# Input product of an encoder layer: gating columns first, the four heads as seven block products in two passes

## The chip, the cores and the metric

The kernel runs on one core of a Trainium2 chip. The metric is the device time of one execution in microseconds (us); the median of three runs before is 2069.68 us (2069.62 to 2071.15). Engines are named as the profile names them: PE (TensorE matmuls), PEld (its weight loads), DVE (VectorE), ACT (ScalarE), POOL (GpSimd), SP (SyncE, which issues the DMAs here).

## The reference, cut to what matters

One encoder layer over 1536 tokens (512 of the prompt, 1024 of the sample), width 1024, all in fp32. The change concerns the token mixer and, at its edges, the memory keys and values.

```python
z = rms_norm(x, w) @ w_in                      # 1024 x 3072
q, k, v, g, u, vs = split(z, 4 of 512, 2 of 512)
q, k = rotary(q), rotary(k) / sqrt(128)        # four heads of 128
y = bidir_retention(q, k, v, log_gamma)        # chunks of 128 tokens, state forward and backward
ret_out = silu(g) * layer_norm(y) * ret_gn_w
vs = layer_norm(gelu(vs)) * sgu_norm_w
sgu_out = gelu(u) * (sgu_w @ vs + sgu_b)       # chunks of 128 tokens, four groups
mix = concat(ret_out, sgu_out) @ w_out
x = x + rms_norm(mix, w)                       # then cross attention to a memory, then the FFN
```

## The kernel before, in words

Tokens stand in twelve tiles of 128 (`NT`), the width in eight slices of 128 (`KT`). To keep fp32 accuracy every operand is split into a rounded part `hi` and a rest `lo` (`split`, L135; `split_scaled`, L139: ACT writes `hi`, DVE subtracts for `lo`), and each product is three matmuls, hi·hi, hi·lo, lo·hi (`mm3`, L156). A matmul is 128x128 by 128x512.

The **input product** runs in six chunks of 512 columns: u, vs, then one chunk for each head (its q, k, v, g). A tile of a chunk takes 8 x 3 = 24 matmuls (`z_half`, L234). Tiles 0 to 3 of the u chunk run while the first loads arrive (L243 to L257), then tiles 4 to 7, then `chunk_tiles` (L315) goes tile by tile. The whole transposed x stays on the chip in split form (`xp`, `xu`), and the weights of the next chunk are loaded during the current one.

Work that follows a tile is written as generators: `post_vs` (L346) for the gating, `ret_tile` (L403) for the forward part of retention, `ret_back` (L455) for the backward part, in which a step per tile runs from the last tile to the first. They stand in the list `side`, and `advance` (L183) runs each by one step. `chunk_tiles` calls `advance` twice per tile, once for each half:

```python
            z_half(ps, t, 0)
            ...
            advance()
            z_half(ps, t, 1)
            ...
            g = post(i, t, ps)
            next(g, None)
            advance()
```

so that PE meets the small matmuls of retention after every 12 block matmuls. In `ret_tile` DVE scales the tile by `rs_x` (L407), POOL and DVE do the rotary part (L415, L417, L420), and DVE scales k twice (L430, L431).

After the heads come the memory's values and keys (L525 to L557, 16 blocks of 24 matmuls, with an `advance` every 12), into which the tail of retention runs, and then `project` (L584), the product with `w_out`, which reads the mixer's result back from `mixT` in DRAM. A scheduler places each engine's instructions, so that an instruction may stand earlier than its line.

Of the kernel before, what the change touches and what calls it, by code (L numbers as in the profile page):

```python
# [82 lines left out]
def encoder_kernel(ctx: ExitStack, tc, x, xTp, xTs, mem, memT, norm_w, w_in, lg, small, sgu_nw, sgu_wT,  # L83
# [37 lines left out]
    lgt = const([P, 8], "lgt")  # L121
# [79 lines left out]

    cB, cC, sinT = FB.units
# [4 lines left out]
    u_units = FC.units + FD.units  # L207
    u_t = [u_units[t // 2][:, (t % 2) * 512 : (t % 2) * 512 + 512] for t in range(NT)]
    wk_units = FE.units

    xp, xu, W = [], [], []

    def xTk(k, t):

        if t < 4:
            p, o = xp[k // 2], (k % 2) * 512 + t * P
        else:
            p, o = xu[k], (t - 4) * P
        return p[0][:, o : o + P], p[1][:, o : o + P]

    def load_pairs(src, n):

        out = []
        for i in range(4):
            r = raw.next()
            nc.sync.dma_start(r, src[i])
            hi, lo = pair(RA)
            for j in range(2):
                s = slice(j * 512, (j + 1) * 512)
                split_scaled(r[:, s], nw(n, 2 * i + j), hi[:, s], lo[:, s])  # L230
            out.append((hi, lo))
            yield out

    def z_half(ps, t, a):  # L234
        for k in range(4 * a, 4 * a + 4):
            mm3(ps, xTk(k, t), half(W, k), k == 0, k == KT - 1)
# [4 lines left out]
    raw.slots = steady + wk_units + u_units  # L241
    first = [mm() for _ in range(4)]
    for i in range(4):  # L243
        rx, rw = raw.next(), raw.next()
        ux, uw = pair(RA), pair(RX, RC)
        xp.append(ux)
        W.append(uw)
        for j in range(2) if i == 0 else (None,):
            s = slice(0, D) if j is None else slice(j * 512, (j + 1) * 512)
            nc.sync.dma_start(rx[:, s], xTp[i][:, s])  # L250
            nc.sync.dma_start(rw[:, s], w_in[0, i][:, s])
        for j in range(2):
            s, k = slice(j * 512, (j + 1) * 512), 2 * i + j
            split_scaled(rx[:, s], nw(PRE_MIX, k), ux[0][:, s], ux[1][:, s])
            split(rw[:, s], uw[0][:, s], uw[1][:, s])
            for t in range(4):
                mm3(first[t], xTk(k, t), half(W, k), k == 0, k == KT - 1)  # L257

    ss_x = const([P, NT], "ss_x")

    def x_stats(t0, t1):
        for t in range(t0, t1):
            r = raw.next()
            nc.sync.dma_start(r, x[t])
            A.activation(r, r, AF.Square, accum_out=ss_x[:, t : t + 1])
        s = slice(t0, t1)
        V.tensor_scalar_mul(ss_x[:, s], ss_x[:, s], 1.0 / D)
        rsqrt(rs_x[:, s], ss_x[:, s])

    def u_out(t, ps):  # L270
        A.activation(u_t[t], ps, AF.Gelu_apprx_tanh, scale=rs_x[:, t : t + 1])

    x_stats(0, 4)
    raw.slots, raw.i = steady + wk_units, -1
    for t in range(4):
        u_out(t, first[t])
    first = [mm() for _ in range(4)]
    for k in range(KT):
        r = raw.next()
        nc.sync.dma_start(r, xTs[k])  # L280
        hi, lo = pair(RB, RC)
        split_scaled(r, nw(PRE_MIX, k), hi, lo)
        xu.append((hi, lo))
        for i in range(4):
            mm3(first[i], xTk(k, 4 + i), half(W, k), k == 0, k == KT - 1)
    x_stats(4, 8)
    for i in range(4):
        u_out(4 + i, first[i])
    x_stats(8, NT)
    raw.slots, raw.i = steady, -1  # L290
    nc.sync.dma_start(swT, sgu_wT)
    nc.sync.dma_start(snB, sgu_nw.partition_broadcast(P))
    nc.sync.dma_start(cosT, cst[:, C_COS : C_COS + 512])
    nc.sync.dma_start(sinT, cst[:, C_SIN : C_SIN + 1024])
    nc.sync.dma_start(lgt, lg.partition_broadcast(P))
    colc = const([P, 4], "colc")
    nc.sync.dma_start(colc, cst[:, C_COL : C_COL + 4])


    ss_m = const([P, 4], "ss_m")  # L300
# [199 lines left out]
    for h in range(4):  # L500
        for t0, n in SEQS:
# [11 lines left out]
            if h == 3 and t0 == 0:  # L513
                for p in xp:
                    free(*p)
# [784 lines left out]
```

## Time and profile before, and how to read it

| | before |
|---|---|
| median of 3 runs | 2069.68 us |
| profiled execution: time | 2064.9 us |
| profiled execution: span | 2063.1 us |
| mean granted TensorE clock | 0.998 |
| PE busy | 2030.0 us (98%) |
| DVE / ACT / POOL busy | 1162.3 / 853.7 / 656.2 us |
| input product, first matmul to the first of `project` | 6.0 to 592.8 us, memory keys and values included |

Matmuls are pipelined: a row's duration is longer than the distance to the next start, so the cost of one is read from start to start. A busy PE is not a PE at its peak. A row that ends in brackets says how long the engine sat idle before it and what released it. In groups, "xN | busy, mean ns | idle before, releaser" gives the count, the summed and mean duration, and idle time just before.

### The profile page before, as it was taken

How to read it: one execution, taken by the hardware profiler on the slowest of the kernel's cores; microseconds unless marked ns; L12 is line 12 of the kernel's file. 1: busy time of each engine (PE TensorE's matmuls, PEld its weight loads, DVE VectorE, ACT ScalarE, POOL GpSimd, SP SyncE). 2: the span in 40 equal slices, each digit the busy share in tenths (PEclk: the TensorE clock that was granted, in tenths of full speed). 3: DMA queues.
4: the chain of work that ended last, by engine and by line, in shares of the span. 5: the costliest groups of instructions: out<-in, count | busy, mean ns of one | idle time of the engine just before them, and what ended most of it. 6: DMA issues, size and time to landing. Idle time of an engine off the chain costs nothing. (4 is left out here: it accounts for less than half of the span.)

```text
span 2063.1 us, 28521 instructions
## 1 busy us (share of the span) xinstructions
PE 2030.0 (98%) x10442; PEld 1800.3 (87%) x10442; DVE 1162.3 (56%) x2132; ACT 853.7 (41%) x1663; POOL 656.2 (32%) x597
## 2 busy tenths in 40 slices
PE   8999999999999999999999999999999999999998
PEld 7788888888788888888888999999999999788887
DVE  4235566675424354463667555657565656845756
ACT  7623222233324443353445444445444444433432
POOL 0011122221022200002336666766676664000102
PEclk9999999999999999999999999999999999999999
DMA  8411101023643322242457434445444344845653
GB/s 327 125 38 59 47 17 47 25 60 121 204 133 143 123 92 72 72 143 93 143 184 217 128 109 132 123 127 167 132 116 128 104 129 156 278 144 200 226 179 134
DMA packets 158749, 268.12 MB, mean 130 GB/s; under 512 B 13200, under 2 KB 97552, under 8 KB 158608
## 3 DMA queue, kind: packets, MB, share of 16 engines
q1 hardware_dynamic: 158608, 266.30, 40.5%
q8 instruction: 82, 1.34, 0.3%
q14 instruction: 59, 0.48, 0.1%
HBM read 194.81 MB, written 71.44 MB: 129 GB/s over the span
## 5 line engine op out<-in xcount | busy, mean ns | idle before, releaser
L137 DVE TENSOR_TENSOR ra<-fa,ra 128x512 fp32r<-128x512 f32 (+1 forms) x168 | 166.0, 992 | 124.5 <-ACT ra L136 123.0
L157 PE MATMUL mm<-rx,ra 128*128 128x384 f32 (+1 forms) x600 | 214.6, 358 | 10.5 <-ACT rx L136 6.0
L159 PE MATMUL mm<-rx,ra 128*128 128x384 f32 (+1 forms) x600 | 211.0, 352 | 0.0
L158 PE MATMUL mm<-rx,ra 128*128 128x384 f32 (+1 forms) x568 | 198.0, 349 | 0.0
L136 ACT ACTIVATE ra<-fa 128x512 fp32r<-128x512 f32 (+1 forms) x168 | 107.1, 642 | 177.7 <-PE mm L158 147.6
L137 DVE TENSOR_TENSOR ra<-ra,ra 128x512 fp32r<-128x512 f32 x154 | 147.1, 956 | 52.9 <-ACT ra L136 52.4
L157 PE MATMUL mm<-rc,ra 128*128 128x384 f32 (+1 forms) x504 | 173.0, 343 | 3.2 <-ACT rb L1041 3.2
L158 PE MATMUL mm<-rc,ra 128*128 128x384 f32 (+1 forms) x504 | 172.5, 342 | 0.0
L159 PE MATMUL mm<-rc,ra 128*128 128x384 f32 (+1 forms) x504 | 172.1, 341 | 0.0
L172 POOL TENSOR_TENSOR rs<-rq,neg_half 128x1 f32<-128x1 f32 x96 | 57.9, 604 | 358.8 <-DVE rq L171 301.1
L136 ACT ACTIVATE ra<-ra 128x512 fp32r<-128x512 f32 x154 | 97.1, 631 | 140.5 <-PE mm L158 136.3
L157 PEld LDWEIGHTS mm<-rx,ra 128*128 128x128 f32 x600 | 113.6, 189 | 17.3 <-ACT rx L136 6.0
L159 PEld LDWEIGHTS mm<-rx,ra 128*128 128x128 f32 x600 | 113.4, 189 | 6.5
L158 PEld LDWEIGHTS mm<-rx,ra 128*128 128x128 f32 x568 | 107.1, 189 | 4.8 <-DVE rx L137 0.4
L415 POOL TENSOR_TENSOR fe<-fe,fb 128x128 f32<-128x128 f32 x96 | 51.2, 553 | 181.6 <-DVE fe L407 165.7
L1061 POOL TENSOR_TENSOR rb<-rb,rb 128x384 f32<-128x384 f32 x66 | 96.1, 1463 | 24.9 <-DVE rb L1049 18.1
L157 PEld LDWEIGHTS mm<-rc,ra 128*128 128x128 f32 x504 | 94.8, 188 | 6.7 <-ACT rb L1041 4.2
L159 PEld LDWEIGHTS mm<-rc,ra 128*128 128x128 f32 x504 | 94.6, 188 | 2.7
L158 PEld LDWEIGHTS mm<-rc,ra 128*128 128x128 f32 x504 | 95.0, 188 | 2.0
L157 PE MATMUL mm<-rx,rb 128*128 128x512 f32 x208 | 88.2, 424 | 0.1
L593 POOL TENSOR_TENSOR rx<-fa,rx 128x1024 fp32r<-128x1024 f32 x6 | 14.4, 2404 | 212.6 <-PE sm L731 191.2
L159 PE MATMUL mm<-rx,rc 128*128 128x512 f32 x196 | 76.8, 392 | 0.0
(474 smaller groups left out, 5568.8 us busy)
## 6 DMA issues: line engine op xcount, KB each, us to landing
hs<-rb SPq DMA_DIRECT2D x154, 192.0 KB, 2.4
fb<-hs SPq DMA_DIRECT2D x42, 704.0 KB, 4.2
fa<-in_wgu_dram SPq DMA_DIRECT2D x44, 512.0 KB, 4.0
ra<-in_wgu_dram SPq DMA_DIRECT2D x44, 512.0 KB, 3.6
rx<-in_wd_dram SPq DMA_DIRECT2D x77, 256.0 KB, 4.8
fa<-in_w_in_dram SPq DMA_DIRECT2D x20, 512.0 KB, 4.6
fa<-mixT SPq DMA_DIRECT2D x12, 512.0 KB, 3.6
fc<-x1d SPq DMA_DIRECT2D x12, 512.0 KB, 3.9
```

What stands on the lines that cost most here:

```text
L136: A.activation(hi, src, AF.Copy)
L137: V.tensor_tensor(lo, src, f32(hi), op=ALU.subtract)
L157: T.matmul(ps, lhsT=a[0], rhs=b[0], start=first, stop=False, skip_group_check=more)
L158: T.matmul(ps, lhsT=a[0], rhs=b[1], start=False, stop=False, skip_group_check=more)
L159: T.matmul(ps, lhsT=a[1], rhs=b[0], start=False, stop=last, skip_group_check=more)
L172: G.tensor_tensor(out, t, neg_half[:, :w], op=ALU.pow)
L415: G.tensor_tensor(t2q[:, s], zq[:, 1 - s], sinT[:, o : o + 64].unsqueeze(1).broadcast_to([P, 2, 64]), op=ALU.mult)
L593: G.tensor_tensor(a[1], r, f32(a[0]), op=ALU.subtract)
L1061: G.tensor_tensor(c[n], c[n], gated[n], op=ALU.mult)
```

## The change

The gating columns u and vs become one chunk of 1024 columns. Tiles 0 to 3 run while the loads arrive, into all eight PSUM banks; tiles 4 to 11 follow one at a time with the six matmuls of a slice in pairs (as `project` does), their x tile loaded and split one tile ahead. The split weights of both columns stay on the chip, x does not.

For the heads, x is scaled by its norm, taken in pairs of tiles by halves of the width (blocks a11 to a22), and four block sums are made by POOL; the seven left blocks of each of six pairs are written to DRAM (`make_S`). Then two passes of two heads each run seven products (`ORDER`) over six pairs: 42 units of 12 matmuls per pass. A unit loads its left block from DRAM and splits it (`fetch_z`, `split_z`); `right_z` builds the right block of the next product from quarters of `w_in` that are loaded again each time, through two landing slots (`z_land`). Results are added up in SBUF. In the second pass every other left block's `lo` is made by POOL.

Retention of a pass's two heads runs during what follows: heads 0 and 1 in the second pass, heads 2 and 3 in the memory's keys and values. `point` stands in for `advance`: three after every two units of the second pass, and one every six matmuls in the memory stage, with a new tile at every second point. DVE gives up the scaling of z and the two scalings of k (to ACT), and one of two operations in `ret_back`.

```diff
+    for k in range(KT):
+...
+        split(rx[:, o : o + 512], xf[:, 0:512], xf[:, 512:D])
+        for i in range(2):
+            s = slice(i * 512, (i + 1) * 512)
+            split_scaled(rw[:, s], nw(PRE_MIX, k), W[k][0][:, s], W[k][1][:, s])
             for t in range(4):
+                mm3(first[t][i], (xf[:, t * P : (t + 1) * P], xf[:, 512 + t * P : 640 + t * P]),
+                    [q[:, s] for q in W[k]], k == 0, k == KT - 1)
+    def make_S(j, xs):
+...
+            V.tensor_tensor(r, r, row.unsqueeze(1).broadcast_to([P, KT, P]), op=ALU.mult)
+...
+        G.tensor_tensor(s1, a21, a22, op=ALU.add)
+        G.tensor_tensor(s2, s1, a11, op=ALU.subtract)
+        G.tensor_tensor(s3, a11, a21, op=ALU.subtract)
+        G.tensor_tensor(s4, a12, s2, op=ALU.subtract)
+        yield
+        for n, src in ((1, a11), (2, a12), (4, a22), (5, s1), (6, s2), (7, s3), (3, s4)):
+            nc.sync.dma_start(Sd[n, j], src)
+    ORDER = (1, 5, 6, 4, 7, 2, 3)
+    z_units = [(hp, n, tp) for hp in (1, 2) for n in ORDER for tp in range(6)]
+...
+    z_land = Ring([FA.units[2][:, i * 512 : (i + 1) * 512] for i in range(2)])
+    def split_z(i):
+...
+            if i >= 42 and i % 2:
+                A.activation(hi, Sq[i], AF.Copy)
+                G.tensor_tensor(lo, Sq[i], f32(hi), op=ALU.subtract)
+            else:
+                split(Sq[i], hi, lo)
+    def right_z(hp, n, k):
+        def load(kb, cb):
+            r = z_land.next()
+            nc.sync.dma_start(r, w_in[hp, 4 * kb + k][:, cb * 512 : (cb + 1) * 512])
+            return r
+...
+        if n == 1:
+            A.activation(st, load(0, 0), AF.Identity, scale=n0)
+            split(st, hi, lo)
+        elif n in (5, 6, 4):
+            V.scalar_tensor_tensor(st, load(int(n != 5), int(n != 4)), n0 if n == 5 else n1, st,
+                                   op0=ALU.mult, op1=ALU.subtract)
+            split(st, hi, lo)
+        elif n == 7:
+            r, o = load(1, 1), load(0, 1)
+            A.activation(o, o, AF.Identity, scale=n0)
+            V.scalar_tensor_tensor(r, r, n1, o, op0=ALU.mult, op1=ALU.subtract)
+            split(r, hi, lo)
+        else:
+            split_scaled(load(1, int(n != 2)), n1, hi, lo)
+    for t in range(4, NT):
+...
+                for i in range(2):
+                    T.matmul(pss[i], lhsT=ak[x0], rhs=W[k][x1][:, i * 512 : i * 512 + 512],
+                             start=st and k == 0, stop=sp and k == KT - 1)
-        V.tensor_scalar_mul(z, ps[:, 0:384], rs_x[:, t : t + 1])
-        V.tensor_scalar_mul(kfb[:, 0:P], k, kfs)
-        V.tensor_scalar_mul(kfb[:, P : 2 * P], k, kbs)
+        A.activation(kfb[:, 0:P], k, AF.Identity, scale=kfs)
+        A.activation(kfb[:, P : 2 * P], k, AF.Identity, scale=kbs)
-            V.tensor_scalar(yp, yp, mv[:, 0:1], rs, op0=ALU.subtract, op1=ALU.mult)
-            V.tensor_tensor(yp, yp, sg, op=ALU.mult)
+            V.scalar_tensor_tensor(yp, yp, mv[:, 0:1], sg, op0=ALU.subtract, op1=ALU.mult)
+            A.activation(yp, yp, AF.Identity, scale=rs)
+    for ui, (hp, n, tp) in enumerate(z_units):
+        fetch_z(ui + 2)
+        split_z(ui + 1)
+...
+        if ui in (37, 79):
+...
+            feed[0] = ret_feed(hp)
+        ps = mm()
+        s = Sq.pop(ui)
+        for k in range(4):
+            mm3(ps, (s[:, k * P : (k + 1) * P], s[:, 512 + k * P : 640 + k * P]), Tq[hp, n, k], k == 0, k == 3)
+            if k % 2:
+                credit += 0.75 if ui > 37 else 0.25
+                if credit >= 1.0:
+                    credit -= 1.0
+                    point()
+        if tp < 4 and then[0] < 3:
+            right_z(*then, tp)
+...
+            nxt = load_split(wk[d + 1], (c0[2], rb[8]) if d % 2 == 0 else c0[0:2])
-    project(mixT, w_o, POST_MIX, x, x1d, BLOCKS, Ring([(RA.units[8], RB.units[8]), (RX.units[8], RC.units[8])]),
+    project(mixT, w_o, POST_MIX, x, x1d, BLOCKS, Ring([(RA.units[8], RB.units[8]), (RC.units[2], RC.units[8])]),
```

What the change moves is seen in the order of the instructions. PE, in the retention of one head, before: L157 to L159 are block matmuls of the head's chunk, L435 to L446 the state and score matmuls of one tile, L450 its output, L424 and L425 the transposes of another.

```order
L159 MATMUL mm_2503<-rx2_12_74,rc2_9_71 128x512
L435 MATMUL sm_2548<-fe_17_79,fb_14_76 128x128
L437 MATMUL sm_2548<-fe_17_79,fb_14_76 128x128
L439 MATMUL sm_2548<-fb_14_76,fd_16_78 128x128
L446 MATMUL sm_2523<-fd_16_78,fe_17_79 128x128
L157 MATMUL mm_2556<-rx0_10_72,rb0_4_66 128x512
```

Twelve block matmuls stand from the last of these rows to the output L450 of the same tile. PE in the second pass of the change: L503 is the score of a tile, L149 to L151 block matmuls of a unit, L507 the output of that tile, L481 and L482 the transposes of the next, L532 a backward step.

```order
L503 MATMUL sm_2418<-fc_15_77,fe_17_79 128x128
L149 MATMUL mm_2433<-rx1_19_1357,rc1_8_70 128x512
L150 MATMUL mm_2433<-rx1_19_1357,rc1_8_70 128x512
L151 MATMUL mm_2433<-rx1_19_1357,rc1_8_70 128x512
L149 MATMUL mm_2433<-rx1_19_1357,rc1_8_70 128x512
L150 MATMUL mm_2433<-rx1_19_1357,rc1_8_70 128x512
L151 MATMUL mm_2433<-rx1_19_1357,rc1_8_70 128x512
L532 MATMUL sm_2467<-fe_17_79,fc_15_77 128x128
L507 MATMUL sm_2418<-rc0_20_1383,fe_17_79 128x128
L481 MATMUL sm_2483<-ident_141,fe_17_79 128x128
L482 MATMUL sm_2483<-ident_141,fe_17_79 128x128
```

Here six block matmuls stand between the score and the output; elsewhere in the pass it is twelve, about as often.

DVE in the heads before, one tile's forward work among the backward work of another sequence (L476 to L486):

```order
L407 TENSOR_SCALAR fe_17_79<-mm_2899,rs_x_150 128x384
L476 SCALAR_TENSOR_TENSOR fd_16_78<-sm_2962,dec_1239,fd_16_78 128x128
L417 TENSOR_TENSOR fe_17_79<-fe_17_79,fb_14_76 128x256
L482 SCALAR_TENSOR_TENSOR fb_14_76<-fb_14_76,dec_1239,fd_16_78 128x128
L420 TENSOR_TENSOR fe_17_79<-fe_17_79 128x256
L484 BN_STATS bn6_133_2966<-fd_16_78 128x6
L445 SCALAR_TENSOR_TENSOR fb_14_76<-fb_14_76,dec_1239,sm_2976 128x128
```

DVE in the second pass of the change: L380 and L386 build right blocks from a landed quarter, L136 makes a left block's `lo`, the rest is retention.

```order
L136 TENSOR_TENSOR rc1_8_70<-fb_14_76,rc1_8_70 128x512
L477 TENSOR_TENSOR fe_17_79<-fe_17_79 128x256
L380 SCALAR_TENSOR_TENSOR fa_13_75<-fa_13_75,sml_146 128x512
L502 SCALAR_TENSOR_TENSOR fe_17_79<-fe_17_79,dec_1362,sm_2655 128x128
L505 TENSOR_TENSOR fe_17_79<-sm_2627,fb_14_76 128x128
L474 TENSOR_TENSOR fe_17_79<-rc0_20_1383,fb_14_76 128x256
L510 SCALAR_TENSOR_TENSOR fd_16_78<-sm_2655,dec_1362,fd_16_78 128x128
L477 TENSOR_TENSOR fe_17_79<-fe_17_79 128x256
L386 SCALAR_TENSOR_TENSOR fa_13_75<-fa_13_75,sml_146 128x512
L136 TENSOR_TENSOR rc1_8_70<-fe_17_79,rc1_8_70 128x512
L505 TENSOR_TENSOR fe_17_79<-sm_2672,fb_14_76 128x128
```

The score's mask (L505, between L503 and L507 on PE) now stands in one queue behind the right blocks (L380, L386), which wait for a DMA, and the left blocks' `lo` (L136), for which the next units wait.

## Rows read from the trace of the kernel before

**Rows 1.** The page: span, and busy time of each engine.

```profile
span 2063.1 us, 28521 instructions
PE 2030.0 (98%) x10442; PEld 1800.3 (87%) x10442; DVE 1162.3 (56%) x2132; ACT 853.7 (41%) x1663; POOL 656.2 (32%) x597
```

**Rows 2.** Busy time by stage: gating, heads, inside the heads, memory; last clock, DMA.

```profile
core 0: us, PE busy (x) PEld busy (x) DVE busy (x) ACT busy (x) POOL busy (x), PEclk, DMA share, GB/s
6.00:165.00 159.00, 155.38 (x734) 128.66 (x735) 63.59 (x138) 90.87 (x138) 15.30 (x16) 0.99 0.47 165
165.00:505.00 340.00, 338.27 (x1800) 286.51 (x1799) 212.62 (x669) 97.65 (x303) 74.14 (x136) 1.00 0.15 44
200.00:425.00 225.00, 225.00 (x1206) 191.46 (x1205) 140.79 (x447) 59.00 (x194) 49.67 (x93) 1.00 0.11 32
505.00:592.60 87.60, 85.35 (x382) 68.96 (x381) 38.34 (x81) 27.95 (x38) 9.12 (x10) 1.00 0.63 204
```

**Rows 3.** Timeline of PE, block matmuls: first and last of 37 starts (start, duration).

```profile
59.74 0.39 PE L157 MATMUL mm<-rx,rb 128*128 128x512 f32 x1
...
67.90 0.39 PE L157 MATMUL mm<-rx,rc 128*128 128x512 f32 x1
```

**Rows 4.** Timeline of PE where the vs chunk's first gating matmuls start.

```profile
84.67 0.39 PE L159 MATMUL mm<-rx,ra 128*128 128x512 f32 x1
88.45 1.69 PE L362 MATMUL sm<-fe,fb 128*128 128x128 f32 x8 [3.40 <-ACT fe L356]
89.80 0.77 PE L157 MATMUL mm<-rx,ra 128*128 128x512 f32 x1
...
92.43 0.39 PE L157 MATMUL mm<-rc,ra 128*128 128x512 f32 x1
```

**Rows 5.** Timeline of PE, all idle rows from 500 to 592.

```profile
516.64 0.46 PE L475 MATMUL sm<-fb,fd 128*128 128x128 f32 x2 [0.60 <-DVE fb L482]
523.70 0.46 PE L475 MATMUL sm<-fb,fd 128*128 128x128 f32 x2 [0.62 <-DVE fb L482]
527.20 0.49 PE L475 MATMUL sm<-fb,fd 128*128 128x128 f32 x2 [0.17 <-DVE fb L482]
534.45 0.30 PE L465 MATMUL sm<-ident,fd 128*128 128x128 f32 x1 [0.73 <-DVE fd L490]
```

**Rows 6.** Groups of DVE and ACT up to 640 us.

```profile
L407 DVE TENSOR_SCALAR fe<-mm,rs_x 128x384 f32<-128x384 f32 x48 | 29.6, 617 | 54.3 <-PE mm L159 54.3
L430 DVE TENSOR_SCALAR fb<-fe,dec 128x128 f32<-128x128 f32 x24 | 6.7, 279 | 0.3
L137 DVE TENSOR_TENSOR rx<-fa,rx 128x1024 fp32r<-128x1024 f32 x16 | 19.4, 1220 | 15.7 <-ACT rx L136 15.4
L137 DVE TENSOR_TENSOR rx<-fe,rx 128x512 fp32r<-128x512 f32 x4 | 2.6, 685 | 0.0
L141 DVE SCALAR_TENSOR_TENSOR ra<-fa,sml,ra 128x512 fp32r<-128x512 f32 x12 | 8.7, 742 | 5.8 <-ACT ra L140 5.8
L140 ACT ACTIVATE ra<-fa,sml 128x512 fp32r<-128x512 f32 x12 | 8.4, 722 | 4.2 <-DMA fa<-in_xTp_dram 3.7 <-PE mm L158 0.4
```

**Rows 7.** DVE and POOL side by side in the FFN: timeline, then two groups.

```profile
1702.93 0.69 DVE L137 TENSOR_TENSOR ra<-ra,ra 128x512 fp32r<-128x512 f32 x1
1704.46 1.29 POOL L881 TENSOR_TENSOR ra<-ra,fa 128x512 f32<-128x512 f32 x1
1704.94 1.36 DVE L137 TENSOR_TENSOR ra<-fa,ra 128x512 fp32r<-128x512 f32 x1
...
L137 DVE TENSOR_TENSOR ra<-fa,ra 128x512 fp32r<-128x512 f32 x164 | 161.1, 986 | 119.5 <-ACT ra L136 118.0 <-DMA ra<-in_wgu_dram 1.4
L593 POOL TENSOR_TENSOR rc<-fa,rx 128x1024 fp32r<-128x1024 f32 x6 | 14.4, 2396 | 22.6 <-ACT rx L592 22.6
```

**Rows 8.** DMA issues of 256 KB: count, size, median us to landing.

```profile
rx<-in_wd_dram SPq DMA_DIRECT2D x77, 256.0 KB, 4.8
fa<-kTd SPq DMA_DIRECT2D x8, 256.0 KB, 2.9
```

More of the change, by code (lines that the diff above doesn't have):

```diff
@@ L206, in encoder_kernel @@
     snB = cC[:, 512:1024]
[L207 to L236, printed above, removed]
+    rsx_row = [sinT[:, 0:512], sinT[:, 512:D], cosT]
+    W = [(RA.units + RB.units)[2 * k : 2 * k + 2] for k in range(KT)]
+    x_r = Ring([RC.units[0:2], (RC.units[2], RC.units[6]), RC.units[7:9]])
+    u_r, vs_r, m_r = carve(FE.units + FC.units[2:] + FD.units[2:], (512, 4), (512, 4), (512, 2))
+    sums_x = [u[:, i * 512 : (i + 1) * 512] for u in FD.units[0:2] for i in range(2)]
+    LEFTS = ("A11", "A12", "S4", "A22", "S1", "S2", "S3")
+    Sd = {(n, j): dram.tile([P, 512], F32, tag=f"xs{n}_{j}", name=f"xs{n}_{j}") for n in range(1, 8) for j in range(6)}
+    rsxd = dram.tile([NT, P], F32, tag="rsxd", name="rsxd")
     nc.sync.dma_start(sml, small)
@@ L240, in encoder_kernel @@
     steady = raw.slots
[L241 to L255, printed above, removed]
+    raw.slots = steady + FE.units + FC.units + FD.units
@@ L270, in u_out @@
[L270 to L300, printed above, removed]
@@ new lines, in encoder_kernel, with point, to_memory @@
+    feed = [None, 0]
+    def point():
+        feed[1] += 1
+        g = next(feed[0], None) if feed[0] is not None and feed[1] % 2 == 0 else None
+        if g is not None:
+            next(g)
+        advance()
+        if g is not None:
+            side.append(g)
+        elif feed[0] is not None and feed[1] % 2 == 0:
+            feed[0] = None
+    rsrow = cC[:, 0:512]
+    mT = []
+    mem_r, wvs = {}, []
+    def to_memory(step):
+        if step == 0:
+            raw.slots, raw.i = FA.units[0:2], -1
+            mem_r["rb"] = Part([big(f"rb{i}", F32R) for i in range(3)])
+            mem_r["rc0"] = Part([big("rc0", F32R)])
+        elif step <= 4:
+            i = step - 1
+            r = raw.next()
+            nc.sync.dma_start(r, memT[i])
+            hi, lo = mem_r["rb"].units[2 * i : 2 * i + 2]
+            for j in range(2):
+                s = slice(j * 512, (j + 1) * 512)
+                split_scaled(r[:, s], nw(MEM, 2 * i + j), hi[:, s], lo[:, s])
+            mT.append((hi, lo))
+        elif step <= 8:
+            c0 = mem_r["rc0"].units
+            wvs.append(load_split(wv[0, step - 5], (c0[0:2], (c0[2], mem_r["rb"].units[8]), RX.units[0:2],
+                                                    (RX.units[2], RX.units[6]))[step - 5]))
@@ L539, in encoder_kernel @@
             nc.sync.dma_start(vd[t][:, c * 512 : c * 512 + 512], st)
-        for p in w:
-            free(*p)
+    rb, c0 = mem_r["rb"].units, mem_r["rc0"].units
+    places = [RX.units[2 * d : 2 * d + 2] for d in range(4)] + [RC.units[3:5], (RC.units[5], RX.units[8])]
     w_o = []
-    nxt = load_split(wk[0], pair(RB))
+    nxt = load_split(wk[0], c0[0:2])
     for d in range(KT):
@@ L557, in encoder_kernel @@
         nc.sync.dma_start(kTd[d], st)
+    while feed[0] is not None:
+        point()
+    w_o.append(load_split(w_out[6], c0[0:2]))
     drain()
-    for p in mT:
-        free(*p)
+    RA = Part([big(f"ra{i}", F32R) for i in range(3)])
+    RB = mem_r["rb"]
+    RC = Part(mem_r["rc0"].tiles + [RC.tiles[1], big("rc2", F32R)])
+    w_o.append(load_split(w_out[7], RC.units[6:8]))
+    raw.slots, raw.i = steady, -1
     BLOCKS = ((0, 1, 2, 3), (11, 10, 9, 8), (7, 6, 5, 4))
@@ L1238, in _layout @@
              for h in range(4)]
-    chunks = [w[:, 2048:2560], w[:, 2560:3072]] + heads
+    chunks = [w[:, 2048:3072]] + [np.concatenate(heads[i : i + 2], axis=1) for i in (0, 2)]
     def kpairs(m):
@@ L1261, in _layout @@
         "norm_w": c(nwv),
-        "w_in": c(np.stack([kpairs(m) for m in chunks])),
+        "w_in": c(np.stack([m.reshape(KT, P, D) for m in chunks])),
         "lg": c(a["ret_log_gamma"][0].reshape(8)),
```

344 lines of the change are left out of this document (221 added, 123 removed).

## The prediction, written before the changed kernel was run

> **What bounds the kernel now.** I read the page first. PE is busy 2030.0 of 2063.1 us, 98%, and DVE, the next engine, 56% [rows 1]: no engine but PE can bound the whole. The stages say the same [rows 2]. The heads have PE busy 338.27 of 340 us, and between 200 and 425 us all of 225.00; the memory's keys and values lose 2.25 us, the gating stage 3.62. What the clock granted is 0.99 to 1.00 in all of them, so the price of a matmul is constant. The timeline of PE gives it: 36 intervals from 59.74 to 67.90 are 8.16 us, 0.2267 us for a 128x512 matmul [rows 3]. So the time is the number of block matmuls times that, plus the small matmuls, plus what PE waits. The change takes from the first, leaves the second, and may add to the third.
>
> **Removed: matmuls.** The input product has 6 chunks x 12 tiles x 24 = 1728 block matmuls. Afterwards the gating columns have 12 x 48 = 576, the heads 2 passes x 42 units x 12 = 1008, together 1584. So 144 go: 144 x 0.2267 = **-32.6 us**, on the path, since PE is the path. The state, score and transpose matmuls stay the same in number.
>
> **Removed: the gating handover.** Where the vs chunk's first tiles are done, PE sits 3.40 us until ACT has delivered, and the six block matmuls from 89.80 to 92.43 take 0.438 us each [rows 4], nearly twice 0.2267: after the idle time the clock is at its lower level for a while. That is 3.40 + 6 x (0.438 - 0.227) = 4.7 us. In the new order the gating of the first four tiles runs beside a 48-matmul tile (10.9 us). I keep 1 us for it: **-3.6** (bounds -4.7 and 0).
>
> **Moved: retention.** In the memory stage of before, PE waits four times for retention, 0.60 + 0.62 + 0.17 + 0.73 = 2.12 us in all [rows 5], in about 13 visits spaced by 12 matmuls. I take these out (**-2.1**) and price all visits anew. The change makes about 96 visits (24 tiles of two heads in each stage, score and output each), half of them with 6 block matmuls in front in place of 12, that is 1.36 us of cover in place of 2.73 (the order of PE shows both). DVE's step behind a score takes the same time, but its queue holds right blocks and left blocks' `lo` ahead of it. The lower bound is 0, as between 200 and 425 us, where the visits cost nothing [rows 2]; the upper one is 48 short visits x 0.73, the largest row of [rows 5], or 35 us. The memory stage, the only one where visits wait, gives 2.12 / 13 = 0.16 us; I take that for all of them: 96 x 0.16 = **+15.4**, half in each stage. This is the term I know least.
>
> **Moved: DVE's work in the second pass.** DVE is busy 212.62 us in the heads of before [rows 2]; without its sixteen x splits (19.4 us, L137 128x1024 [rows 6]) that is 193.2 / 48 = 4.03 us per tile and head. It gives up L407 (0.62), the two scalings of k (0.28 each, L430 and its neighbour) and one more pass over 128x128 (0.28 by the same row): 2.57 left, x 24 tiles = 62 us. The blocks add 41 subtractions (0.685, L137 128x512), 24 products with subtraction (0.742, L141) and 36 additions into the accumulators (0.685 again, though one operand is in PSUM): 70.6. Together 132 us. PE has 504 x 0.2267 = 114.3 plus the retention's small matmuls; those are (340 - 1.7 - 1152 x 0.2267) / 48 = 1.61 us per tile from [rows 2], 38.6 for 24 tiles: 152.9, and with half of the waits above 160.6. In the FFN a subtraction beside POOL takes 1.36 instead of 0.69 us, and 164 of them average 986 ns instead of 685 [rows 7]. POOL now makes 21 of the left blocks' `lo` (1.29 each), so I add 0.30 x 65 two-input operations: 152 us. DVE would be 95% full in a pass that must also answer PE in order. Taken: **+3** (0 if it stays off the path; the third rival is the other end). ACT gets 66 roundings (0.722, L140 [rows 6]) besides 97.65 / 48 = 2.0 us per tile [rows 2] and the three operations it takes over (0.62 + 2 x 0.28): 111 us, covered. POOL's four block sums per pair, 24 x 2.4 us (L593 [rows 7]) = 58, lie in a gating stage of 159 us where POOL is busy 15.30 [rows 2]: covered; if not, the heads start late by what is missing of the first pair's 9.6 us.
>
> **Added: right blocks through two slots.** A product needs four right blocks, made during the six units of the one before: 6 x 12 x 0.2267 = 16.3 us in the first pass, about 23 in the second (160.6 / 7). Most need one load. The product n = 7 needs two, so that the next block's loads wait until both slots are free: landing + 0.722 (ACT) + 0.742 (DVE) + 0.722 (ACT) + 0.685 (DVE) = landing + 2.9. A landing of 256 KB takes 4.8 us in the FFN and 2.9 in the heads of before [rows 8]. The first pair can come early, three follow: 3 x 7.7 + 2.9 = 26.0 us against 16.3, 9.7 late in the first pass, 3 in the second, by 4.8; 20.3, 4 late and 0, by 2.9. The heads moved 44 GB/s [rows 2]; now a pass moves (42 + 32) x 0.262 MB = 19.4 MB, 170 GB/s in the first pass, nearer to the gating stage's 165, so I lean to 4.8: **+7** for both (bounds 0 and the second rival's price).
>
> **Moved: the start of `project`.** Its first split goes to a buffer that the last key block still reads, so that POOL's `lo` (2.4 us for 128x1024 [rows 7]) starts when PE's last use ends, behind which lie only some four matmuls: 2.4 - 0.9 = **+1.5** (bounds 0 and 2.4).
>
> **Sum.** -32.6 - 3.6 - 2.1 + 15.4 + 3 + 7 + 1.5 = -11.4. The profiled execution took 2064.9 us, 1.8 more than its span and 4.8 under the median of the runs. So it would take 2053.5, and the median 2069.7 - 11.4 = **2058 us**. A change of 0.2% (4.1 us) is about what a measurement of this kernel can tell from none. The range of this case by itself, with the retention's waits between 6 and 25 us, is 2049 to 2067.
>
> **The rivals.**
> *First, the waits stay hidden.* Visits cost nothing, as between 200 and 425 us [rows 2], DVE and the loads keep up: -32.6 - 3.6 + 1.5 = -34.7, or 2035 us. For it: DVE has 20 us of slack in the second pass by busy time. Against it: the memory stage has waits even with 12 matmuls of cover [rows 5].
>
> *Second, slower: a right block's load holds DVE's queue.* DVE takes its instructions in the order shown, and behind the subtraction that waits for the landing stand the left blocks' `lo` of the next unit and the additions that free PSUM banks. Then the landing is not beside PE's work but stops it. Place: product n = 7, in each pass; price: three links x 4.8 us x 2 = 29 in place of 7, and the time is 2080. It decides where 256 KB take about 4.8 us to land; at 2.9 [rows 8] the queue stands for at most 17 us, part of it covered. For it: the order of DVE. Against it: a landing is at most two units of the first pass, and the left blocks are fetched two units ahead. Idle times of the size of 3.40 us would cost the clock as well, as in [rows 4].
>
> *Third, DVE becomes the bound of the second pass through POOL.* The row shows a subtraction that began 0.48 us into POOL's 1.29 and took 1.36 [rows 7], as if it had only begun when POOL was done. The rule would be that DVE loses the whole of POOL's time, not 0.30 us per operation. POOL then takes 21 x 1.29 + 48 x (74.14 / 136 = 0.55 [rows 2]) = 53 us from DVE where all of it collides, and two thirds, 36, by the share of DVE's work that reads two operands in SBUF: 132 + 36 to 53 = 168 to 185, in the middle 176.5, or 23.6 over PE's 152.9. The 3 us and this pass's half of the waits (7.7) go into it: 2058 - 10.7 + 23.6 = 2071, no change. Against it: 986 ns is far from 685 + 1290 [rows 7]. The Trainium skill, page "SBUF — State Buffer", section "Who interferes with whom", states that a VectorE instruction with two inputs in SBUF contends with a GpSimd instruction that reads SBUF, and that whoever issues second blocks for the whole instruction. The trace agrees for the one pair of rows (1.36 against 0.69 us); how often it happens, no row of before shows.
>
> **How the numbers follow.** The forecast's case has 0.48, the first rival 0.20 (the memory stage's waits speak against a clean pass), the second 0.19, the third 0.13. Faster by over 0.2% means under 2065.5: the first rival and nearly all of the forecast's case, **0.66**; within 0.2%: most of the third and the forecast's upper edge, **0.13**; slower: the second, and the worst end of the third, **0.21**. Range: half of the first rival and half of the second left out, 2036 to 2079.
>
> **What would show it.** In the changed profile PE's busy time falls by about 33 us, and its idle time rises from some 33 to some 55. Right if the idle rows of PE lie at scores and outputs (L503, L507) and backward steps (L532) in the second pass and the memory stage, each some tenths of a us, with some us at the product n = 7 of the first pass, and none of 3.4 us in the gating stage. The first rival shows as a second pass of about 153 us without idle rows; the second as idle rows of several us before L149 or L380's DVE work, with releaser a DMA of `w_in`; the third as DVE over 95% busy in the second pass and a mean of the left blocks' `lo` well above 685 ns. A clock under 0.99 in the heads, PE's busy time falling by another amount than 33, or waits at a place not named here (the heads' first unit, the memory's loads) would make the prediction wrong in its steps.

## The result, and the profile after

The change made the kernel slower: 2090.08 us median of four runs against 2069.65 of the kernel before beside it, a ratio of 1.0103 (95% interval 1.0085 to 1.012). The prediction was 2058, with a range of 2036 to 2079. The profiled execution of the changed kernel took 2092.05 us, that of before 2064.9; so the two traces differ by 27.2 us in their spans, the medians by 20.4.

The page of the changed kernel, against [rows 1]:

```profile
span 2090.3 us, 29212 instructions
PE 2016.9 (96%) x10298; PEld 1782.0 (85%) x10298; DVE 1248.4 (60%) x2163; ACT 961.1 (46%) x1967; POOL 744.1 (36%) x654
```

PE has 144 instructions less (10442 before), as the sum had it, but its busy time fell by 13.1 us only, and its idle time rose from 33.1 to 73.4. Where, the windows by stage say: gating, first pass, second pass, memory. Against [rows 2], the columns to look at are the length, PE's busy time and, behind the five engines, the granted clock and the share of the DMA engines.

```profile
core 0: us, PE busy (x) PEld busy (x) DVE busy (x) ACT busy (x) POOL busy (x), PEclk, DMA share, GB/s
6.00:196.60 190.60, 158.43 (x703) 130.20 (x704) 85.03 (x155) 77.05 (x124) 52.57 (x39) 0.91 0.78 218
196.60:311.00 114.40, 112.62 (x506) 92.56 (x505) 78.95 (x135) 61.45 (x130) 15.17 (x15) 1.00 0.51 150
311.00:487.00 176.00, 167.41 (x885) 136.72 (x884) 150.37 (x369) 111.43 (x320) 80.53 (x105) 1.00 0.45 133
487.00:614.00 127.00, 123.60 (x679) 102.69 (x677) 87.22 (x261) 71.30 (x208) 32.87 (x58) 1.00 0.50 156
```

The loss lies in the gating stage. It has the same 576 block matmuls as before. Counted in the timeline of PE, the first block matmul of the heads starts at 159.29 us before and at 196.64 now: **+37.4 us**. From there to the end of the memory's keys and values it was 433.5 us and is 417.4: **-16.1**, where the matmuls taken out give -32.6. The rest, `project` on, takes 1476.2 in place of 1470.3: **+6.0**. Sum 27.2 (each part rounded), the difference of the spans.

The timeline of PE, its five largest idle rows in the gating stage, then the two at the start of `project`:

```profile
68.11 7.22 PE L409 MATMUL mm<-ra,rc 128*128 128x512 f32 x24 [16.32 <-ACT fe L263]
102.82 2.07 PE L278 MATMUL sm<-fe,fb 128*128 128x128 f32 x8 [4.14 <-ACT fe L272]
135.06 1.25 PE L278 MATMUL sm<-fc,fb 128*128 128x128 f32 x8 [4.08 <-ACT fc L272]
152.81 1.87 PE L278 MATMUL sm<-fc,fb 128*128 128x128 f32 x8 [3.62 <-ACT fc L272]
169.64 1.65 PE L278 MATMUL sm<-fe,fb 128*128 128x128 f32 x8 [2.68 <-ACT fe L272]
...
615.32 1.20 PE L779 MATMUL mm<-rx,ra 128*128 128x512 f32 x4 [1.27 <-ACT ra L746]
617.76 1.22 PE L779 MATMUL mm<-rx,rb 128*128 128x512 f32 x2 [1.25 <-POOL rb L747]
```

And PE's waits over the gating stage, summed by what ended them (the row of the first matmul, which any version has, is left out):

```profile
PE mm L409 <- ACT fe L263: 16.3, 1, 16.3
PE sm L278 <- ACT fc L272: 8.2, 3, 4.1
PE sm L278 <- ACT fe L272: 7.6, 4, 4.1
```

That is 32.1 us of idle time where before had the 3.40 of [rows 4]: 28.7 more. The other 8.7 of the 37.4 go with a lower granted clock: 0.91 over the stage (0.99 before), and 24 matmuls in 7.22 us behind the 16.32 us pause, 0.30 each in place of 0.2267 [rows 3]. The windows behind the five largest pauses, in which the granted clock is 0.50, hold 18.8 us of PE's work, 3.4 in before; at half speed that is an estimated 9.4 us lost against 1.7, or 7.7 of the 8.7.

What was late at 68 us? ACT's L263, the gelu that empties a PSUM bank of the first four tiles. It stood in ACT's queue behind the split of an x tile (L135) and behind squares of x (L245), which waited for loads. Here is what those loads waited for: SP's queue and ACT's, in order of time. L256 writes the norms of four tiles (`rs_x`) to DRAM in transposed order, 2 KB as 512 words of 4 bytes; L257 loads them again as a row for all partitions; L304 loads a tile of x. L240 loads x for the squares, L248 is the last square of a group.

```profile
28.75 0.39 SPq L256 DMA_DIRECT2D rsxd<-rs_x  x1
29.20 0.50 SPq L240 DMA_DIRECT2D fc<-in_x_dram  x1
41.28 0.33 SPq L257 DMA_DIRECT2D fb<-rsxd  x1
42.18 0.38 SPq L304 DMA_DIRECT2D fc<-in_xTt_dram  x1
```

```profile
43.17 1.06 ACT L248 ACTIVATE fc<-fc 128x1024 f32<-128x1024 f32 x1 [11.04 <-DMA fc<-in_x_dram]
```

```profile
rsxd<-rs_x SPq DMA_DIRECT2D x2, 2.0 KB, 12.6
```

The last row is from the DMA issues of 20 to 70 us: two writes of 2 KB, 12.6 us to landing in the median, more than twice what 256 KB took in [rows 8]. Two causes fit these rows. SP's queue stands at L257 until the write has landed, with the x tiles behind it; SP's waits at L257 add up to 27.0 us in three times (theory A). Or the write itself delays every transfer issued after it: the load of x at 29.20, issued behind the write but *before* SP stood still, also lands only just before 43.17 (theory D). A third candidate, for the later pauses, is POOL, which makes the block sums and also the rsqrt of the gating (L164), ahead of ACT's L272 (theory C). The experiments take these apart.

### The profile page after: what moved, and what is told of

It is laid out like the page before. It is cut to its first block, busy times and chain, and to the rows that moved or that the text cites. A ratio compares the mean times of both kernels' runs of the same rounds, so it can differ in the third digit from the quotient of the medians.

```text
span 2090.3 us, 29212 instructions
## 1 busy us (share of the span) xinstructions
PE 2016.9 (96%) x10298; PEld 1782.0 (85%) x10298; DVE 1248.4 (60%) x2163; ACT 961.1 (46%) x1967; POOL 744.1 (36%) x654
## 5 line engine op out<-in xcount | busy, mean ns | idle before, releaser
L136 DVE TENSOR_TENSOR ra<-fa,ra 128x512 fp32r<-128x512 f32 (+1 forms) x168 | 166.6, 995 | 124.2 <-ACT ra L135 122.6
L135 ACT ACTIVATE ra<-fa 128x512 fp32r<-128x512 f32 (+1 forms) x168 | 107.1, 642 | 179.8 <-PE mm L150 148.0
L136 DVE TENSOR_TENSOR ra<-ra,ra 128x512 fp32r<-128x512 f32 x154 | 146.7, 953 | 53.6 <-ACT ra L135 53.2
L135 ACT ACTIVATE ra<-ra 128x512 fp32r<-128x512 f32 x154 | 97.2, 632 | 144.9 <-PE mm L150 141.4
L164 POOL TENSOR_TENSOR rs<-rq,neg_half 128x1 f32<-128x1 f32 x96 | 60.5, 631 | 277.7 <-DVE rq L163 267.5
L149 PE MATMUL mm<-rx,ra 128*128 128x384 f32 x440 | 148.2, 337 | 5.4 <-ACT rb L1194 3.1
L149 PE MATMUL mm<-rc,ra 128*128 128x384 f32 x440 | 147.8, 336 | 2.8 <-ACT rb L1194 2.8
L151 PE MATMUL mm<-rx,ra 128*128 128x384 f32 x440 | 147.8, 336 | 0.0
L150 PE MATMUL mm<-rx,ra 128*128 128x384 f32 x440 | 147.8, 336 | 0.0
L150 PE MATMUL mm<-rc,ra 128*128 128x384 f32 x440 | 147.4, 335 | 0.0
L151 PE MATMUL mm<-rc,ra 128*128 128x384 f32 x440 | 147.4, 335 | 0.0
L149 PE MATMUL mm<-rx,rc 128*128 128x512 f32 x288 | 116.4, 404 | 0.7 <-ACT rx L135 0.7
L150 PE MATMUL mm<-rx,rc 128*128 128x512 f32 x288 | 112.6, 391 | 0.6 <-DVE rx L136 0.6
L151 PE MATMUL mm<-rx,rc 128*128 128x512 f32 x288 | 112.8, 392 | 0.5 <-DVE rc L136 0.5
L136 DVE TENSOR_TENSOR rx<-fa,rx 128x512 fp32r<-128x512 f32 (+1 forms) x67 | 63.8, 960 | 54.8 <-ACT rx L135 54.5
L135 ACT ACTIVATE rc<-fb 128x512 fp32r<-128x512 f32 (+2 forms) x56 | 52.4, 937 | 88.4 <-PE mm L150 67.7
L149 PEld LDWEIGHTS mm<-rx,ra 128*128 128x128 f32 x440 | 83.1, 189 | 6.5 <-ACT rb L1194 3.8
L149 PEld LDWEIGHTS mm<-rc,ra 128*128 128x128 f32 x440 | 83.0, 189 | 3.8 <-ACT rb L1194 3.8
L150 PEld LDWEIGHTS mm<-rx,ra 128*128 128x128 f32 x440 | 83.2, 189 | 0.0
L151 PEld LDWEIGHTS mm<-rx,ra 128*128 128x128 f32 x440 | 83.2, 189 | 0.0
```

The costliest lines, as they stand in the source:

```text
L135: A.activation(hi, src, AF.Copy)
L136: V.tensor_tensor(lo, src, f32(hi), op=ALU.subtract)
L149: T.matmul(ps, lhsT=a[0], rhs=b[0], start=first, stop=False, skip_group_check=more)
L150: T.matmul(ps, lhsT=a[0], rhs=b[1], start=False, stop=False, skip_group_check=more)
L151: T.matmul(ps, lhsT=a[1], rhs=b[0], start=False, stop=last, skip_group_check=more)
L164: G.tensor_tensor(out, t, neg_half[:, :w], op=ALU.pow)
```

## The experiments

Each experiment is compared with the kernel before on its own chip; us are worked out as the difference of two ratios times 2069.65. A difference of two of these ratios is uncertain by about 0.2%, 4 us.

**1. The row loaded without a wait.** The write stays; the row is loaded from an input, so this version scales x for the heads by other numbers.

```diff
-            nc.sync.dma_start(rsx_row[t0 // 4], rsxd[t0:t1]....partition_broadcast(P))
+            nc.sync.dma_start(rsx_row[t0 // 4], sgu_nw.partition_broadcast(P))
```

> The row of norms (L257) is loaded from sgu_nw, an input of the same size, in place of the value that L256 has just written; L256 stays, so the scaling of x for the heads is left wrong. Theory A (SP's queue is held: L257 waits 27.0 us in three waits for L256 to land, and the loads of x tiles and of the norms stand behind it): the 16.3 us of PE idle at 68 us fall below 8 us, the gating stage (6.1 to 196.6 us) ends 15 to 30 us earlier, the time is 2060 to 2076. Theory B (what holds PE is the transfers themselves, DMA engines 0.75 to 0.9 busy): over 10 us of that idle time stay and the time is over 2083. Theory C (POOL's block sums in front of the rsqrt on POOL): the 16.3 us stay too.

Measured: 2086.75 us, ratio 1.0094 (1.0079 to 1.0109): no change. PE's first pause is 14.16 us still. Theory A, SP's wait, falls. The timelines of SP and ACT in this run show why:

```profile
29.07 0.39 SPq L256 DMA_DIRECT2D rsxd<-rs_x  x1
29.55 0.93 SPq L240 DMA_DIRECT2D fc<-in_x_dram  x2
30.54 0.42 SPq L257 DMA_DIRECT2D fb<-in_sgu_nw_dram  x1
31.00 0.43 SPq L296 DMA_DIRECT2D fb<-in_sgu_wT_dram  x1
```

```profile
42.84 1.06 ACT L245 ACTIVATE fc<-fc 128x1024 f32<-128x1024 f32 x1 [11.19 <-DMA fc<-in_x_dram]
```

SP no longer stands still: it issues everything at once behind the write, and the data still come 13 us later. So theory D, the second of the two causes: the write holds up the transfers issued after it. Theory B, that PE waits for the mass of the transfers, forecast the same for this run.

**2. The row made by PE.** The write and its reload both go; DVE scales the identity by the norms, one matmul with a block of ones spreads them.

```diff
-            nc.sync.dma_start(rsxd[t0:t1].rearrange("t p -> p t"), rs_x[:, s])
-            nc.sync.dma_start(rsx_row[t0 // 4], rsxd[t0:t1]....partition_broadcast(P))
+        for i in range(4):
+            V.tensor_scalar_mul(r[:, i * P : (i + 1) * P], ident, rs_x[:, 4 * g + i : 4 * g + i + 1])
+        ps = sm()
+        T.matmul(ps, lhsT=ones, rhs=r, start=True, stop=True)
+        A.activation(r, ps, AF.Copy)
```

> The row of norms is made on the chip (DVE scales the identity, one fp32 matmul with ones, ACT copies), so that the 2 KB write of single words (L256) and its reload (L257) are both gone; the result is the same. Theory A: as e1 or better, the gating stage 20 to 35 us shorter, the time 2056 to 2072. Theory B: over 10 us of idle time stay at the first wait, the time over 2080. If this is much faster than e1, the write itself (DMA engines busy for 12.5 us with 2 KB) cost as well as the wait for it.

Measured: 2061.16 us, ratio 0.997 (0.9957 to 0.9982), 27.5 us below the change and already below the kernel before. The first pause is gone; the heads start at 168.28 us. Theory B, which had over 2080 us for this run, falls. But this edit moves the other transfers as well, so two more runs isolate the write, from both sides.

**3. The write alone taken away**, from experiment 1 (no L256, the row from an input):

> As e1 (the row is loaded from sgu_nw), and the 2 KB write of single words (L256) is left out as well; the scaling of x for the heads stays wrong. Theory D (the write itself keeps the DMA engines for some 12 us, during which the loads issued behind it wait; the order in SP's queue is not the point): the 14.2 us of idle time of e1 fall below 2 us, the first unit starts at 163 to 173 us in place of 191.5, the time is near e3's, 18 to 28 us below e1 (2059 to 2069 where before is at 2066). Theory E (what shortened e3 was its other order of transfers, not the missing write): within 6 us of e1.

Measured: 2057.33 us, ratio 0.9948 (0.9932 to 0.9964), 30 us below experiment 1; the heads start at 165.66.

**4. The write alone put back**, to experiment 2, with no reader:

```diff
+            nc.sync.dma_start(rsxd[t0:t1].rearrange("t p -> p t"), rs_x[:, s])
```

> As e3 (norm row made by PE), and the three 2 KB writes of single words are issued again, with no reader and nobody waiting for them; the result is the same. Theory D: 12 to 25 us slower than e3, a first idle time of 8 to 16 us at the first gating tile, under 40 GB/s in the 12 us after each of the first two writes. Theory E: within 4 us of e3.

Measured: 2086.22 us, ratio 1.009 (1.007 to 1.011), 25 us above experiment 2, with a first pause of 12.41 us. Theory D holds from both sides, theory E falls. The windows of 28 to 40 us, in order of experiments 1, 3, 4 and 2, show it in the last number, GB/s:

```profile
28.00:40.00 12.00, 12.00 (x54) 9.94 (x54) 0.00 (x0) 2.30 (x4) 1.03 (x1) 1.00 0.25 27
```

```profile
28.00:40.00 12.00, 12.00 (x55) 9.93 (x54) 2.79 (x4) 5.97 (x10) 1.57 (x2) 1.00 0.85 305
```

```profile
28.00:40.00 12.00, 12.00 (x54) 9.94 (x53) 0.88 (x4) 3.10 (x6) 1.03 (x1) 1.00 0.67 42
```

```profile
28.00:40.00 12.00, 12.00 (x55) 9.93 (x54) 4.54 (x12) 5.66 (x10) 1.57 (x2) 1.00 0.77 289
```

With the write, 27 and 42 GB/s; without, 305 and 289. Three writes of 2 KB cost this kernel 25 to 30 us. The Trainium skill, page "DMA: Bandwidth & Descriptors", section "Rules for kernel authors", states that a non-contiguous last dimension is lowered to one descriptor per element, and advises to rearrange. The runs agree with the advice, and the trace of experiment 1 is in line with the count: behind the write of 512 words it has 529 packets under 512 B, about one a word. These are its DMA packets from 29.5 to 30.5 us and from 30.5 to 41 us:

```profile
DMA packets 531, 0.01 MB, mean 10 GB/s; under 512 B 529, under 2 KB 529, under 8 KB 531
```

```profile
DMA packets 66, 0.27 MB, mean 26 GB/s; under 512 B 0, under 2 KB 0, under 8 KB 66
```

The small packets are through within 1 us; the slow time comes behind them. That it is the word by word form, and not any write of 2 KB, no run here isolates.

**5. No block sums** (plain blocks are written in their place, so the heads' values are not those of the layer), in the change as it was:

> POOL's four block sums per pair are left out (a plain block is written to DRAM in place of each sum), so the four sums of x are not computed. Theory C (the sums stand in front of the rsqrt on POOL, and SP's writes of the sums wait for POOL): the later gating waits of 4.1, 4.1, 3.6 and 2.7 us mostly go, the time falls by 8 to 20 us, the 16.3 us stay. Theory A: the waits at 135, 153 and 170 us may go, but the one at 103 us (behind L257 in SP's queue) stays with the 16.3 us; the time falls by 5 to 12 us. Theory B: no change beyond 4 us, the bytes are the same.

Measured: 2073.57 us, ratio 1.0039 (1.0025 to 1.0054), 13 us below the change. The first pause stays with 12.06 us, and so does one of 4.00 at 99 us; of the others 1.06 and 3.56 are left. So the sums cost time of their own, beside the writes of the norms.

**6. Sums on DVE.** First a small edit to experiment 2: the first fetch of `project` ahead of the load of w_out's last block.

```diff
+    first_a = fetch_a(mixT, 0, a_mix)
     w_o.append(load_split(w_out[7], RC.units[6:8]))
```

> As e3, with the first fetch of project put ahead of the load of w_out's last block (which is needed ten us later). If the 2.7 us of idle time at the start of project and the lower clock behind it come from the late load of mixT, both shrink and the time falls by 2 to 5 us; if they come from the buffer that the last key block still reads (POOL's lo, as the prediction had it), the time falls by less than 1 us.

Measured: 2061.31 us, ratio 0.9968 (0.9956 to 0.998): not told from experiment 2. The pause before the first matmul of `project` is gone in its trace, and the trace's span is 4.3 us shorter, which the medians don't bear out. Inconclusive. Then the four sums:

```diff
-        G.tensor_tensor(s1, a21, a22, op=ALU.add)
+        V.tensor_tensor(s1, a21, a22, op=ALU.add)
...
```

> As e7, with the four block sums per pair on DVE in place of POOL. If POOL's sums are what SP's writes, and behind them the loads of the first right blocks and ACT's queue, wait for, the waits of 5.7 and 2.2 us in the gating stage of e3 fall below 3 us in all, and the time falls by 4 to 8 us against e7; if they are not, it stays within 2 us, or rises by up to 4 through DVE's own queue (24 sums of some 0.7 us).

Measured: 2044.25 us, ratio 0.9883 (0.9866 to 0.9899): 17.6 us below experiment 6's first part (the profiled executions differ by 13.0, 11.0 of it before the heads start), and **24 us below the kernel before**. More than the 4 to 8 us that were expected. All pauses of the gating stage are gone, and the heads start at 157.23 us, 2 us earlier than before. The path is seen in the traces of experiment 2 (SP's writes L337, the load's arrival on ACT) and of the early fetch (PE's pause, SP's waits from 60 to 150 us):

```profile
105.75 11.93 SPq L337 DMA_DIRECT2D xs<-fd  x8
117.73 0.42 SPq L379 DMA_DIRECT2D fa<-in_w_in_dram  x1
```

```profile
121.15 0.72 ACT L388 ACTIVATE fa<-fa,sml 128x512 f32<-128x512 f32 x1 [11.83 <-DMA fa<-in_w_in_dram]
```

```profile
124.84 2.07 PE L289 MATMUL sm<-fc,fb 128*128 128x128 f32 x8 [5.53 <-ACT fc L283]
```

```profile
SPq L337 <- POOL fd L332: 12.8, 6, 3.6
SPq L337 <- POOL fd L331: 5.9, 4, 3.0
```

SP's eight writes wait for POOL's sums; the load of the first right block (L379) stands behind them; ACT takes it into its queue ahead of the gating's L283 (L272 in the change) and sits 11.83 us; PE waits for L283. To see how much of the gain goes this way, POOL still makes the sums, but plain blocks are written:

> As e7, with the four block sums still made by POOL but not written: plain blocks are written to DRAM in their place, so SP's writes no longer wait for POOL, while POOL's queue is as full as before (the heads' values are wrong). If e8 gained because SP's queue no longer waited for POOL's sums (the loads of the first right blocks stand behind those writes, and ACT and DVE wait for them), the time is near e8's, 10 to 18 us below e7 (a ratio to before of 0.988 to 0.992); if it gained because POOL's rsqrt no longer stands behind the sums, the time stays within 4 us of e7 (a ratio of 0.995 to 0.999).

Measured: 2055.32 us, ratio 0.993 (0.9914 to 0.9947), 8 us below the early fetch, between the two expectations. So about half of the 17.6 us goes through SP's queue, give or take the 4 us. The other half fits POOL's rsqrt (L164) standing behind the sums: PE has idle rows of 3.77 and 0.98 us left there, and ACT, which releases the first, waits for POOL.

```profile
84.25 0.72 ACT L283 ACTIVATE fe<-fe,rs 128x512 f32<-128x512 f32 x1 [9.97 <-POOL rs L164]
```

That part was not tried by itself.

**7. The heads.** Points after twelve matmuls instead of six, in the change as it was:

```diff
-            if k % 2:
-                credit += 0.75 if ui > 37 else 0.25
+            if k == 3:
+                credit += 1.5 if ui > 37 else 0.5
```

> In the second pass the points of retention are called after 12 block matmuls (one or two at a time) in place of 6; the scheduler still places the instructions. If the cover of 6 matmuls is what PE's idle 8.0 us of this pass come from, they fall to 3 or less and the time by 4 to 6 us; if DVE's queue (L505 behind right blocks and lo) is, the idle time stays at 6 to 10 us and the time within 3 us.

Measured: 2087.03 us, ratio 1.0102 (1.0087 to 1.0117): no change, and PE's waits in the second pass are 11.8 us, not less. This does not clear the cover, because the edit does not give twelve throughout. Counted in the timelines of PE, only 10 of the 26 outputs of that pass have twelve block matmuls or more between score and output; the others have one to eleven, since two points now come together. In the change it is 8 with twelve and 18 with six or seven, so not "about as often". Over both runs one output in 18 with twelve waited, and 9 of 34 with fewer. So short cover may be part of these waits; what it is worth was not shown. The next two start from the version with the sums on DVE. One load for n = 7:

> As e8, with one load in place of two for the right blocks of product n = 7 (the other quarter of w_in is left out of these blocks, so their values are wrong). If the two loads through two slots cost what the prediction gave them (7 us), the time falls by 5 to 9 us; if they lie beside PE's work, as the trace of e8 has it (no idle row of PE in the first pass), by less than 2 us.

Measured: 2044.53 us, ratio 0.9896 (0.988 to 0.9913): no change. All `lo` of the second pass on DVE:

> As e8, with the lo of every left block of the second pass on DVE (21 subtractions of some 0.7 us moved from POOL, where they took 1.3 us); the result is the same. If POOL's splits slow DVE by more than they relieve it (third rival), the time falls by 2 us or more; if DVE's queue is what the scores wait for, 14 us more of work in it make the idle 8.3 us of the second pass 10 to 20, and the time rises by 3 to 12 us; within 2 us if neither decides.

Measured: 2040.54 us, ratio 0.9879 (0.9865 to 0.9894). Against the run beside it (2044.53) it is 4 us lower, against the version that it starts from (0.9883) 0.8 us, and the intervals overlap: not slower, and not told from it. So a longer queue of DVE, 14 us more of work in the pass, did not lengthen the time.

## Why the prediction was wrong, point by point

By its own signs the prediction is wrong in its steps: it asked for no idle row of 3.4 us in the gating stage, and there are rows of 16.32, 4.14, 4.08 and 3.62.

**Matmuls, -32.6: right in number.** The heads and the memory stage have 1392 block matmuls in the trace, 1536 before.

**The gating stage, -3.6: here it failed.** "In the new order the gating of the first four tiles runs beside a 48-matmul tile. I keep 1 us for it" (bounds -4.7 and 0); the stage measured +37.4. The handover itself was not what was wrong: with both causes below gone (experiment 6) no pause is left and the heads start 2.1 us earlier than before. Two costs of the same stage were put at nothing. The three writes of the norms and their reloads were part of the change and got no term at all; they cost 25 to 30 us (experiments 1 to 4). And "POOL's four block sums per pair [...] covered" compared busy times (58 us of sums in 159 us), not queues: SP's writes wait for the sums, and loads, ACT and PE stand behind them; 17.6 us (experiment 6). The 58 us were too many even so: the price of 2.4 us is for 128x1024 [rows 7], a block is 128x512, and POOL took 1.26 us for one. Half the busy time did not help.

The bound of 0 on that side was unfounded, and the trace of before could have shown it: before has one such write, of the memory's norms (`rsd`, L311, 512 words, at 69.22 us). These are the DMA issues of 63 to 69, 69 to 70 and 73 to 76 us, and ACT's wait behind them:

```profile
fa<-in_w_in_dram SPq DMA_DIRECT2D x3, 512.0 KB, 4.6
rsd<-rs_m SPq DMA_DIRECT2D x1, 2.0 KB, 8.5
fa<-in_w_in_dram SPq DMA_DIRECT2D x3, 512.0 KB, 8.5
```

```profile
81.92 1.06 ACT L136 ACTIVATE rx<-fa 128x1024 fp32r<-128x1024 f32 x1 [4.68 <-DMA fa<-in_w_in_dram]
```

The write took 8.5 us to land, and the loads issued 4 to 7 us behind it took 8.5 in place of 4.6. Whether the pause of 3.40 us in [rows 4], which follows at 88.45, has to do with it, no run tried.

**Retention's visits, DVE, right blocks: -2.1 + 15.4 + 3 + 7 = +23.3 in the sum, +16.5 measured** (32.6 - 16.1). Of these, 9.0 are idle time of PE (12.8 us against 3.9 before, summed over the idle rows). The other 7.5 lie mostly in the steps into, through and out of the visits, counted from start to start; block matmuls that follow one another without a wait take only 1.1 us more in all, beyond 0.2267 each, than they did before. The sum did not have these steps. The waits are where they were expected, in the second pass at L507 and L481:

```profile
PE sm L507 <- DVE fe L505: 3.8, 6, 0.9
PE sm L481 <- ACT fe L524: 2.5, 5, 1.2
PE sm L522 <- ACT fd L547: 1.5, 4, 0.5
PE sm L532 <- DVE fe L539: 0.2, 1, 0.2
```

They make 8.0 us there and 1.3 + 1.0 + 0.5 + 0.3 in the memory stage, where the sum had 7.7 each. "Half of them with 6 block matmuls in front" was too few: by the timelines of PE it is 37 of the 48 outputs, 20 of them in the memory stage. What the waits of the second pass come from stays open: neither the cover (experiment 7, first part) nor DVE's queue (its last part) was shown to be it.

**Right blocks, +7: about 0.** PE waits 1.8 us in the whole first pass, and the version with one load is no faster. A quarter of `w_in` landed in 3.0 us there, the lower of the two values of [rows 8], though the pass moved 150 GB/s.

```profile
fa<-in_w_in_dram SPq DMA_DIRECT2D x27, 256.0 KB, 3.0
```

With that the second rival (DVE's queue held by a landing) falls too. DVE does stand at the landings of the first pass, 6.9 us at n = 7 (L386) and 2.8 at L380, but PE had work in front of it. The time was on this rival's side, 2080, by luck: another mechanism, in another stage.

**DVE beside POOL, +3, and the third rival.** DVE is busy 150.4 us in the second pass (152 expected), which is luck in part: 13.5 us of its rows there split the memory's operands, work that the sum did not have in this pass, while a `lo` of a right block (first row) or of a left one is slowed by 0.08 to 0.09 us on the mean, not by 0.30, against the 0.685 of [rows 6]:

```profile
L136 DVE TENSOR_TENSOR rx<-fa,rx 128x512 fp32r<-128x512 f32 x16 | 12.0, 760 | 0.8 <-ACT rx L135 0.8
L136 DVE TENSOR_TENSOR rc<-fb,rc 128x512 fp32r<-128x512 f32 x14 | 10.8, 774 | 2.7 <-PE sm L482 2.3 <-ACT rc L135 0.4
```

The rival's rule holds where the two meet in the order that it needs. Two meetings, POOL and then DVE:

```profile
414.35 1.29 POOL L360 TENSOR_TENSOR rx<-fb,rx 128x512 fp32r<-128x512 f32 x1
415.01 1.17 DVE L136 TENSOR_TENSOR rx<-fa,rx 128x512 fp32r<-128x512 f32 x1
...
450.74 1.29 POOL L360 TENSOR_TENSOR rc<-fb,rc 128x512 fp32r<-128x512 f32 x1 [0.64 <-ACT rc L359]
450.85 1.72 DVE L136 TENSOR_TENSOR rc<-fb,rc 128x512 fp32r<-128x512 f32 x1
```

Both subtractions end 0.54 us behind the end of POOL's, as the one of [rows 7] did (0.55). Of the 37 in the pass six went so, 0.93 to 1.72 us long; eleven others lay beside a POOL operation without loss, seven of them begun ahead of it and three beside POOL's one-column rsqrt (L164), and twenty beside none. DVE did not become the bound, and taking POOL's 21 subtractions away gained at most the 4 us of the last run. The Trainium skill's rule on two SBUF inputs (page "SBUF — State Buffer", section "Who interferes with whom") agrees with the six; it says nothing of how often the two meet.

**The start of `project`, +1.5: +6.0 in the trace.** Two pauses, 1.27 and 1.25 us, and slower matmuls behind them. The second pause, POOL's `lo`, is the expected one; the first, the late load of `mixT`, was not foreseen. The granted clock behind them is 0.50 from 617.3 to 620.6 us.

**Slips in the working.** ACT's terms as listed give 125 us, not 111 (the two scalings of k were left out); it was busy 111.4. The first rival's sum leaves out the -2.1. For the right blocks +7 lies nearer to the case of 2.9 us (4) than to the one of 4.8 (12.7), to which the text leaned. None of these decided the result.

Without the two omissions the forecast's sign holds: the version with neither the writes nor POOL's sums is 24 us faster than before (19.7 between the two profiled spans), about twice the 11.4 of the sum.

## What to carry to other kernels

Price every DMA that a change adds, small ones above all, and look for one of its form in the trace of before: a write of 2 KB word by word cost more than a 256 KB load, and not to the one who waited for it but to the transfers issued behind it. Where a new producer is off the critical path by busy time, follow its reader in the DMA-issuing queue: what is queued behind that reader (loads, the engine that takes them, what that engine does next) is what waits. A stage that keeps its arithmetic still has to be forecast if its transfers change.

## What the runs showed of the hardware

A transposed write of 512 words (2 KB) took 12.6 us to land, and in the 12 us around it all transfers together moved 27 to 42 GB/s, against 289 to 305 without it. Removing the wait for it changed nothing; removing the write gave 30 us. In what way it holds the others stays open: its small packets were through within 1 us, and the DMA engines' busy share in the window was 0.25 in one run and 0.67 in another. All these transfers were issued by SP; whether the write would hold those of another issuer was not tried.

PE's granted clock fell to 0.50 of full speed, the lower of its two levels (1.2 GHz), within the 16.32 us pause, as a window of the changed kernel shows:

```profile
56.00:60.00 4.00, 0.00 (x0) 0.00 (x0) 0.00 (x0) 0.49 (x1) 0.00 (x0) 0.50 0.71 195
```

The stage's mean of 0.91 goes with some 8.7 us on top of the pauses themselves.

A DVE subtraction of 128x512 with both operands in SBUF that began behind a POOL operation of the same kind ended 0.54 to 0.55 us after it, 1.17 to 1.72 us long in place of 0.685; one that began first took 0.67 to 0.69.
